# Attention heads in one hybrid decoder layer: where scores, values and filler work stand in TensorE's order, and how rotated queries and keys reach their tiles

## The chip, the cores and the metric

The kernel runs on one core of one Trainium2 chip. The metric is the device time of one execution in microseconds (us). Inputs and outputs lie in the chip's DRAM, the on-chip memory is called SBUF, and TensorE adds up its products in PSUM. The engines are named as in the profile: PE (TensorE), DVE (VectorE), ACT (ScalarE), POOL (GpSimd) and SP (SyncE). Here SP issues every DMA, one after the other in program order.

## The reference, cut to what matters

One decoder layer for 1024 tokens and width 1024. Its first sub-layer runs two mixers on the same input x and merges them; cross-attention and a feed-forward network follow. The part that the change touches is the second mixer, differential attention with 8 heads, two 64-wide query and key components per head, and 128-wide values:

```python
dq = rope(da_q, positions);  dk = rope(da_k, positions)      # (.., 8 heads, 2, 64)
lam = exp(sum(lam_q1*lam_k1)) - exp(sum(lam_q2*lam_k2)) + lam_init
# per head and block of 128 queries:
s = einsum('qcd,kcd->cqk', q, k) * 64**-0.5,  -inf above the diagonal
p = softmax(s, -1);  a = p[0] - lam * p[1];  o = a @ v
o = head_rms_norm(o, da_norm_w) * (1 - lam_init)
y_b = o @ w_proj_b
mix = (g_a * y_a + g_b * y_b) @ w_mix_out        # y_a: output of the first mixer times w_proj_a
```

## The kernel before

Every large product is made in three TensorE passes: an f32 operand is split into a high part (`bh`, `whi`) and a rest (`bl`, `wlo`), and high by high, rest by high and high by rest are added. ACT or POOL writes the high part, DVE or POOL the rest (`to_hi` and `to_lo`, lines 139 to 149); all matmuls are recorded at line 152.

PE follows the order in which the program is written (`manual_schedule`); the other engines' orders come from a scheduler. The written order is made by a small queue of generators, `Weave`. A filler (a piece of work that depends on nothing in the attention) is added to the queue and gives up control after each *quantum*, in most fillers three matmuls of 512 columns. The attention's own generator yields a number, and `W.pump(n)` then writes n quanta of filler behind what the attention has just written. `W.ensure(name)` writes filler until the named one is complete; `W.later` calls a function some quanta on. A head yields 60 quanta in all.

Per head, four groups g of 256 queries are done: `scores(h, g)` writes the products of Q with K and with klo (the rest of K) into PSUM tiles `sp`; DVE copies them into `e` with mask and row maximum (lines 679 and 682), turns the maximum into the bias of the exponential (L686), ACT takes the exponential and its sum, DVE inverts the sum and multiplies one half by -lam (L691), POOL scales one half of `e` (L692) and DVE joins both (L693). `values(h, g)` transposes `e` on PE (`tp`), ACT and DVE split the result into `ath` and `atl`, and PE multiplies with the values into `op`. Lines 736 to 750 then do the RMS norm: `of` is the scaled output (DVE, L741), a sum of squares `ss` goes through PE five quanta later, ACT takes Ln and Exp of it into `rt`, POOL multiplies, and a DMA writes `of` to `oT_d` in DRAM. `values(h, g-1)` follows `scores(h, g)`, and `values(h, 3)` stands directly behind `values(h, 2)`.

The fillers are listed per head in `FILL`: "P" the projections of the next head (`g_rope` for Q and K, per pair of heads also V), "G" a gate (`g_gate`), "q" and "v" cross-attention products that are spilled to DRAM (`spill`, tile `ev`, ACT at L765), "h" the loads of the first mixer's result hT into the buffers that held x (`g_load`, 16 DMAs of 512 KB), and "Y" its output projection y_a (eight `g_ya`, 16 quanta each). `g_rope` rotates a 128x512 block in tiles `raw` and `rot` (tag "rope", four buffers, shared with `gt`, `ev` and `vt`) and writes it from SBUF to SBUF into Q, K and klo, by DMAs of 64 partitions (L633). Each of Q, K and klo has two tiles and one buffer per tile. Before a head's first scores, `ensure` writes out what is left of its Q and K.

Behind the attention the last quanta of y_a are drained, while oT is loaded from `oT_d` and split (`load_slab`, 8 slabs of 512 KB); its products with w_proj_b (`yb`) come next.

Of the kernel before, what the change touches and what calls it, by code (L numbers as in the profile page):

```python
# [12 lines left out]
F = mybir.dt.float32  # L13
R = mybir.dt.float32r
I32 = mybir.dt.int32
AF = mybir.ActivationFunctionType
OP = mybir.AluOpType
# [13 lines left out]
BIG = 1e30  # L31
NEG = -1e30
# [3 lines left out]
NRAW = 4  # L36
AHEAD_T = 80
NG_A = 5
FILL = (("G", "q0", "P", "G"), ("P", "q1"), ("G", "q2", "P", "G"), ("P", "G"), ("G", "q3", "P", "G"), ("P", "G"),
        ("G", "P", "G"), ("h0", "v0", "h1", "v1", "h2", "v2", "h3", "v3", "Y"))  # L40
PUMP_K = 4
PUMP_S = 1
PUMP_T = 2
PUMP_O = 2
# [71 lines left out]
def hybrid_layer(ctx: ExitStack, tc: tile.TileContext, a: dict, out: bass.AP):  # L116
    nc = tc.nc
    V, S, G, PE = nc.vector, nc.scalar, nc.gpsimd, nc.tensor
# [9 lines left out]
    W = Weave()  # L128
# [5 lines left out]
    def to_hi(dst, src, eng=None):  # L134
        if eng is None:
            eng = hi_plan[turn["h"] % len(hi_plan)]
            turn["h"] += 1
        if eng == "s":
            S.activation(dst, src, AF.Copy)  # L139
        elif eng == "g":  # L140
            G.tensor_scalar(dst, src, 1.0, 0.0, op0=OP.mult, op1=OP.add)  # L141
        else:
            V.tensor_copy(dst, src)
# [47 lines left out]
    def g_fm(wsrc, acts, evac, pool=None, w=None):  # L191

        w = w or split_all(load_w(wsrc, pool), 1024, pool)
        for j, (ah, al) in enumerate(acts):
            n = ah.shape[-1]
            acc = acc_tile()
            for k in range(KT):
                mm3(acc[:, :n], cut(w[k // 4], (k % 4) * 128, (k % 4) * 128 + 128), (ah[:, k, :], al[:, k, :]),
                    k == 0, k == KT - 1)
                yield  # L200
            evac(j, acc)
# [38 lines left out]
    hT_d = dr.tile([2, 8, 128, 1024], F, name="hT_d")  # L240
    oT_d = dr.tile([8, 128, 1024], F, name="oT_d")
    g_d = dr.tile([16, 128, 1024], F, name="g_d")
    row_d = dr.tile([2, 32, 128], F, name="row_d")
    dec_d = dr.tile([1, 32], F, name="dec_d")

# [359 lines left out]
    with tc.tile_pool(name="bp", bufs=1, reuse_waits="tile") as B:  # L605
        def g_rope(h, which):


            t_ = 16 + 8 * which + h
            dst = [B.tile([128, 1024], R, tag=f"{'QK'[which]}{c}", name=f"{'QK'[which]}{c}") for c in range(2)]  # L610
            if which == 0:
                res["Q"] = dst
                to = [[(dst[0], 0), (dst[1], 64)], [(dst[0], 64), (dst[1], 0)]]
            else:
                klo = [B.tile([128, 1024], R, tag=f"klo{c}", name=f"klo{c}") for c in range(2)]
                res["K"], res["klo"] = dst, klo
                to = [[(kt, r) for kt in pr for r in (0, 64)] for pr in (dst, klo)]

            def ev(j, acc):
                js = slice(j * 512, (j + 1) * 512)  # L620
                raw = B.tile([128, 512], F, tag="rope", name="raw", bufs=NROPE)
                rot = B.tile([128, 512], F, tag="rope", name="rot", bufs=NROPE)
                S.activation(raw, acc, AF.Identity, bias=bfm[:, t_:t_ + 1])
                V.stream_shuffle(rot, raw, [i ^ 16 for i in range(32)])
                V.tensor_tensor(raw, raw, cosT[:, js], op=OP.mult)
                G.tensor_tensor(rot, rot, sinT[:, js], op=OP.mult)
                V.tensor_tensor(raw, raw, rot, op=OP.add)
                to_hi(rot.bitcast(R), raw, "s")
                V.tensor_tensor(raw.bitcast(R), raw, rot, op=OP.subtract)
                for m, places in zip((rot, raw), to):  # L630
                    for n, (t, r) in enumerate(places):
                        c = n if which == 0 else n // 2
                        dma(t[r:r + 64, js].bitcast(F), m[c * 64:c * 64 + 64])  # L633
            yield from g_fm(a["wfm"][t_], xT, ev)

        def g_vB(pr):
            bvd = B.tile([128, 256], F, tag="bvd", name="bvd", bufs=1)
# [13 lines left out]
            res["V", 2 * pr], res["V", 2 * pr + 1] = (vh[0], vl[0]), (vh[1], vl[1])  # L651

        def addB(h):
            if h % 2 == 0:
                W.add(f"V{h}", g_vB(h // 2))
            W.add(f"Q{h}", g_rope(h, 0))
            W.add(f"K{h}", g_rope(h, 1))

        def scores(h, g, qk):
            out_ = []  # L660
            for i in (2 * g, 2 * g + 1):
                n = (i + 1) * 128
                nch = 1 if n <= 512 else 2
                w0 = ((i + 1 + nch - 1) // nch) * 128
                cuts = [(0, w0)] if nch == 1 else [(0, w0), (w0, n)]
                e = [B.tile([128, 1024], F, tag=f"e{c}", name=f"e{c}", bufs=4 - 2 * c) for c in range(2)]
                mx = B.tile([128, 2], F, tag="mx", name="mx", bufs=3)
                su = B.tile([128, 2], F, tag="ssum", name="ssum", bufs=3)
                for c in range(2):
                    run = None  # L670
                    for j, (c0, c1) in enumerate(cuts):
                        w = c1 - c0
                        sp = sm_tile("sp")
                        qs = slice(i * 128, (i + 1) * 128)
                        mm(sp[:, :w], qk[0][c][:, qs], qk[1][c][:, c0:c1], start=True)
                        mm(sp[:, :w], qk[0][c][:, qs], qk[2][c][:, c0:c1], stop=True)
                        if j < len(cuts) - 1:
                            run = B.tile([128, 1], F, tag="run", name="run", bufs=2)
                            V.tensor_scalar(e[c][:, c0:c1], sp[:, :w], 1.0, None, op0=OP.mult, op1=OP.max,
                                            accum_out=run)  # L680
                        else:
                            V.tensor_tensor_reduce(e[c][:, c0:c1], sp[:, :w], cmask[:, 512 - w:512], scale=1.0,
                                                   scalar=NEG if run is None else run, op0=OP.add, op1=OP.max,
                                                   accum_out=mx[:, c:c + 1])
                        yield PUMP_S
                V.tensor_scalar(mx, mx, -0.125, None, op0=OP.mult)  # L686
                for c in range(2):
                    S.activation(e[c][:, :n], e[c][:, :n], AF.Exp, scale=0.125, bias=mx[:, c:c + 1],
                                 accum_out=su[:, c:c + 1])
                V.reciprocal(su, su)  # L690
                V.tensor_tensor(su[:, 1:2], su[:, 1:2], nlam, op=OP.mult)  # L691
                G.tensor_scalar(e[1][:, :n], e[1][:, :n], su[:, 1:2], 0.0, op0=OP.mult, op1=OP.add)  # L692
                V.scalar_tensor_tensor(e[0][:, :n], e[0][:, :n], su[:, 0:1], e[1][:, :n], op0=OP.mult, op1=OP.add)  # L693
                out_.append(e[0])
            res["a", h, g] = out_

        def values(h, g):
# [40 lines left out]
            to_hi(sqp[0], sq, "g")  # L738
            to_lo(sqp[1], sq, sqp[0], "v")
            of = B.tile([128, 256], F, tag="of", name="of", bufs=1)  # L740
            V.tensor_scalar(of, op_[:, :256], dag[:, h:h + 1], None, op0=OP.mult)  # L741
            def norm():
                ss = sm_tile("ss")
                mm(ss[:, :256], ones, sqp[0], start=True)
# [49 lines left out]
        gates = iter(range(NG_A, 16))  # L794

        def attention():
            for h in range(8):
                for nm in FILL[h]:
                    add_fill(nm, h)
                W.ensure(f"Q{h}")  # L800
                W.ensure(f"K{h}")
                W.pump(PUMP_K)
                qk = (res["Q"], res["K"], res["klo"])
                if h == 0:
                    with tc.issue_after(res["act"]), tc.issue_after(res["act2"]):
                        S.preload_act_table_set("natural_log_exp_and_others")
                for g in range(4):
                    yield from scores(h, g, qk)
                    if g > 0:
                        yield from values(h, g - 1)  # L810
                yield from values(h, 3)

        def g_load(part):
            if part == 0:
# [6 lines left out]
                        hT_d[i, ks, :, h * 512:(h + 1) * 512].rearrange("k p c -> p k c"))  # L821
            yield from ()

        def add_ya():
            for f in range(8):
                W.add(f"ya{f}", g_ya(f))

        def gate(i, pool, tag):
# [17 lines left out]
            dma(g_d[f], gt)  # L846

        def add_fill(nm, h):
            if nm == "G":
                W.add("g", g_gate(next(gates), B, "rope", NROPE))  # L850
            elif nm == "P":
                addB(h + 1)
            elif nm[0] == "h":
                W.add("hT", g_load(int(nm[1])))
            elif nm == "Y":
                add_ya()
            elif nm[0] == "q":
                W.add("q", g_qk(int(nm[1])))
            else:
                W.add("v", g_vo(int(nm[1])))  # L860

        addB(0)
        add_fill("G", 0)
        W.drain()
        for n in attention():
            W.pump(n)
        W.pump(LAG_O)
        W.flush()

# [559 lines left out]
```

## Time and profile before

| | |
|---|---|
| Median of 3 runs | 2286.19 us (2283.52 to 2288.44) |
| Profiled execution | 2285.06 us, its span 2283.3 us |
| Mean granted clock of TensorE | 0.989 |
| PE busy | 2207.3 us (97%) |
| DVE busy | 1421.2 us (62%) |
| ACT busy | 696.4 us (30%) |
| POOL busy | 704.9 us (31%) |

The span runs from the first to the last instruction. Busy time of PE includes matmuls whose modelled ends overlap the next one's start. The attention lies between about 450 and 1125 us of the span.

### The profile page before, as it was taken

How to read it: one execution, taken by the hardware profiler on the slowest of the kernel's cores; microseconds unless marked ns; L12 is line 12 of the kernel's file. 1: busy time of each engine (PE TensorE's matmuls, PEld its weight loads, DVE VectorE, ACT ScalarE, POOL GpSimd, SP SyncE). 2: the span in 40 equal slices, each digit the busy share in tenths (PEclk: the TensorE clock that was granted, in tenths of full speed). 3: DMA queues.
4: the chain of work that ended last, by engine and by line, in shares of the span. 5: the costliest groups of instructions: out<-in, count | busy, mean ns of one | idle time of the engine just before them, and what ended most of it. 6: DMA issues, size and time to landing. Idle time of an engine off the chain costs nothing.

```text
span 2283.3 us, 36224 instructions
## 1 busy us (share of the span) xinstructions
PE 2207.3 (97%) x14109; PEld 2008.0 (88%) x14109; DVE 1421.2 (62%) x2655; ACT 696.4 (30%) x1375; POOL 704.9 (31%) x720
## 2 busy tenths in 40 slices
PE   8999999999999999998999999997999999999997
PEld 8898898887988888886888999997899999999996
DVE  8536645357777676676535486478756665556657
ACT  3322213234454454445232123222211111111122
POOL 7124323233333332334412232245421111111124
PEclk9999999999999999999999999999999999999999
DMA  8322222344263343439733423222211111111122
GB/s 319 102 73 93 83 65 88 127 124 132 63 181 100 81 128 83 108 103 316 254 137 138 177 83 105 81 84 74 65 39 54 47 46 56 56 48 45 56 64 94
DMA packets 97963, 238.47 MB, mean 104 GB/s; under 512 B 12128, under 2 KB 30464, under 8 KB 97792
## 3 DMA queue, kind: packets, MB, share of 16 engines
q1 hardware_dynamic: 97792, 236.16, 32.5%
q8 instruction: 111, 1.82, 0.3%
q14 instruction: 60, 0.49, 0.1%
HBM read 168.92 MB, written 41.98 MB: 92 GB/s over the span
## 4 chain that ended last, share of the span: by engine, by line
PE 51%; DVE 5%; DMA 2%; issue 2%; POOL 1%; ACT 1%; SPq 0%; DVEq 0%; POOLq 0%; ACTq 0%
PE acc L152 32%; PE xb L152 7%; PE xa L152 5%; PE xc L152 5%; DVE wlo L149 1%; DMA vo_d<-ev 1%; PE sp L152 1%; DVE d L1040 1%; PE op L152 1%; DVE z L930 0%; DVE xb L149 0%; PE tp L722 0%; DVE z L926 0%; DVE u L1040 0%; PE tp L1007 0%
## 5 line engine op out<-in xcount | busy, mean ns | idle before, releaser
L141 POOL TENSOR_SCALAR whi<-wraw 128x512 fp32r<-128x512 f32 (+1 forms) x250 | 180.0, 720 | 880.3 <-issue 355.6
L152 PE MATMUL acc<-bh,whi 128*128 128x512 f32 x1024 | 418.1, 408 | 0.4 <-ACT gtok L389 0.4
L149 DVE TENSOR_TENSOR wlo<-wraw,whi 128x512 fp32r<-128x512 f32 (+1 forms) x379 | 306.3, 813 | 160.8 <-ACT whi L139 121.1
L152 PE MATMUL acc<-bh,wlo 128*128 128x512 f32 x1024 | 402.2, 393 | 0.0
L152 PE MATMUL acc<-bl,whi 128*128 128x512 f32 x1024 | 402.0, 393 | 0.0
L139 ACT ACTIVATE whi<-wraw 128x512 fp32r<-128x512 f32 (+1 forms) x252 | 157.4, 626 | 550.9 <-PE acc L152 273.9
L152 PEld LDWEIGHTS acc<-bh,wlo 128*128 128x128 f32 x1024 | 193.6, 189 | 42.5
L152 PEld LDWEIGHTS acc<-bh,whi 128*128 128x128 f32 x1024 | 194.0, 189 | 33.4 <-ACT gtok L389 0.6
L152 PEld LDWEIGHTS acc<-bl,whi 128*128 128x128 f32 x1024 | 194.3, 190 | 32.3
L152 PE MATMUL acc<-whi,bh 128*128 128x256 f32 (+1 forms) x728 | 213.2, 293 | 0.2 <-DVE ev L149 0.2
L152 PE MATMUL acc<-whi,bl 128*128 128x256 f32 (+1 forms) x728 | 205.6, 282 | 0.0
L152 PE MATMUL acc<-wlo,bh 128*128 128x256 f32 (+1 forms) x728 | 205.4, 282 | 0.0
L152 PE MATMUL xb<-xe,whi 128*128 128x256 f32 x1008 | 183.8, 283 | 10.3 <-DVE u L1040 7.4
L149 POOL TENSOR_TENSOR wlo<-wraw,whi 128x512 fp32r<-128x512 f32 (+1 forms) x125 | 174.1, 1393 | 9.8
L152 PEld LDWEIGHTS xb<-xe,whi 128*128 128x128 f32 x1008 | 155.9, 190 | 10.9 <-issue 6.8
L152 PE MATMUL xb<-xe,wlo 128*128 128x256 f32 x504 | 142.5, 283 | 0.0
L152 PEld LDWEIGHTS acc<-whi,bh 128*128 128x128 f32 x728 | 138.7, 190 | 2.0 <-DVE ev L149 0.4
L152 PEld LDWEIGHTS acc<-wlo,bh 128*128 128x128 f32 x728 | 138.7, 190 | 1.6
L152 PEld LDWEIGHTS acc<-whi,bl 128*128 128x128 f32 x728 | 138.6, 190 | 0.0
L1250 DVE SCALAR_TENSOR_TENSOR z<-z,acc 128x512 f32<-128x512 f32 x144 | 98.2, 685 | 53.4 <-PE acc L152 51.8
L152 PE MATMUL xa<-xb,whi 128*128 128x256 f32 x672 | 125.5, 287 | 5.2 <-ACT u L1162 5.2
L152 PE MATMUL acc<-wlo,hidh 128*128 128x512 f32 x320 | 124.7, 390 | 1.4 <-DVE wlo L149 1.4
(315 smaller groups left out, 5205.1 us busy)
## 6 DMA issues: line engine op xcount, KB each, us to landing
wraw<-in_wfm_dram SPq DMA_DIRECT2D x48, 512.0 KB, 3.6
wraw<-in_wg_dram SPq DMA_DIRECT2D x24, 512.0 KB, 3.6
wraw<-in_wu_dram SPq DMA_DIRECT2D x24, 512.0 KB, 3.5
wraw<-in_wd_dram SPq DMA_DIRECT2D x22, 512.0 KB, 3.5
hT_d<-hp SPq DMA_DIRECT2D x16, 512.0 KB, 2.8
g_d<-gt SPq DMA_DIRECT2D x32, 256.0 KB, 2.3
K<-rot SPq DMA_DIRECT2D x64, 128.0 KB, 2.3
klo<-raw SPq DMA_DIRECT2D x64, 128.0 KB, 2.3
```

The costliest lines, as they stand in the source:

```text
L139: S.activation(dst, src, AF.Copy)
L141: G.tensor_scalar(dst, src, 1.0, 0.0, op0=OP.mult, op1=OP.add)
L149: (V if eng == "v" else G).tensor_tensor(dst, src, hi.bitcast(F), op=OP.subtract)
L152: PE.matmul(o, l, r, start=start, stop=stop, skip_group_check=True)
L1040: V.tensor_tensor(dst, x_, y_, op=op)
L1250: V.scalar_tensor_tensor(zs, zs, ALPHA if q == 0 else 1.0, acc, op0=OP.mult, op1=OP.add)
```

## The change

- `values(h, 3)` is written behind `scores(h+1, 0)` of the next head instead of before it; only `values(7, 3)` stands alone at the end.
- `FILL` is dealt out anew: each head gets the quanta of its list, divided by 60, for each quantum that the attention yields (`share`), so that a list is used up about when its head ends. The v fillers move forward to heads 4 to 6, the hT loads and the first half of y_a to head 6, and the second half of y_a to head 7. `values(7, 3)` has a share of 0. Before, the queue stayed full until the end.
- `g_rope` writes `rot` and `raw` into a new DRAM tensor `rq_d` (two DMAs of 128x512 per block), and `load_qk(h)` reads Q, K and klo of a head back by 24 DMAs of 64x512, issued once the previous head's last scores are written.
- The scores are copied with a factor of -0.125 and a minimum, so that L686 goes; -lam is a second operand of POOL's instruction, so that L691 goes; `of` is written by ACT instead of DVE (L741).

```diff
-FILL = (("G", "q0", "P", "G"), ("P", "q1"), ("G", "q2", "P", "G"), ("P", "G"), ("G", "q3", "P", "G"), ("P", "G"),
-        ("G", "P", "G"), ("h0", "v0", "h1", "v1", "h2", "v2", "h3", "v3", "Y"))
-PUMP_K = 4
+FILL_0 = ("P0", "V0", "G0")
+FILL = (("P1", "P2", "q0", "G0"), ("V2", "P3", "q1", "G0"), ("P4", "q2", "G0", "G0"), ("V4", "P5", "q3", "G0"),
+        ("P6", "v0", "G0", "G0", "G0"), ("V6", "P7", "v1", "G0"), ("v2", "v3", "G0", "h0", "h1", "h2", "h3", "Y0"), ("Y4",))
+QUANTA = {"P": 32, "V": 32, "G": 16, "q": 8, "v": 8, "h": 0, "Y": 64}
+PUMPS = 60
...
                 to_hi(rot.bitcast(R), raw, "s")
+                dma(rq_d[h, which, 0][:, js], rot)
                 V.tensor_tensor(raw.bitcast(R), raw, rot, op=OP.subtract)
-                for m, places in zip((rot, raw), to):
-                    for n, (t, r) in enumerate(places):
-                        c = n if which == 0 else n // 2
-                        dma(t[r:r + 64, js].bitcast(F), m[c * 64:c * 64 + 64])
+                dma(rq_d[h, which, 1][:, js], raw)
...
+        def load_qk(h):
+            t = [[B.tile([128, 1024], R, tag=f"{n}{c}", name=f"{n}{c}") for c in range(2)] for n in ("Q", "K", "klo")]
+            for j in range(2):
+                js = slice(j * 512, (j + 1) * 512)
+                for n in range(3):
+                    for c in range(2):
+                        for r in range(2):
+                            part = r if n == 0 else n - 1
+                            dma(t[n][c][r * 64:r * 64 + 64, js].bitcast(F),
+                                rq_d[h, min(n, 1), part][c * 64:c * 64 + 64, js])
+            return t
...
-                V.tensor_scalar(mx, mx, -0.125, None, op0=OP.mult)
...
-                V.tensor_tensor(su[:, 1:2], su[:, 1:2], nlam, op=OP.mult)
-                G.tensor_scalar(e[1][:, :n], e[1][:, :n], su[:, 1:2], 0.0, op0=OP.mult, op1=OP.add)
+                G.tensor_scalar(e[1][:, :n], e[1][:, :n], su[:, 1:2], nlam, op0=OP.mult, op1=OP.mult)
...
-            V.tensor_scalar(of, op_[:, :256], dag[:, h:h + 1], None, op0=OP.mult)
+            S.activation(of, op_[:, :256], AF.Copy, scale=dag[:, h:h + 1])
...
+            late = None
+            qk = load_qk(0)
...
                 for g in range(4):
                     yield from scores(h, g, qk)
-                    if g > 0:
-                        yield from values(h, g - 1)
-                yield from values(h, 3)
+                    if g == 3 and h < 7:
+                        W.ensure(f"K{h + 1}")
+                        qk = load_qk(h + 1)
+                    if late:
+                        if late[1] == 0 and late[0]:
+                            W.ensure(f"V{late[0] // 2 * 2}")
+                        yield from values(*late)
+                    late = (h, g)
+                yield None
+            yield from values(*late)
...
-        for n in attention():
-            W.pump(n)
+        for n in steps:
+            if n is None:
+                h += 1
...
+                share = sum(QUANTA[nm[0]] for nm in FILL[h]) / PUMPS if h < 8 else 0
+                continue
+            left += n * share
+            W.pump(int(left))
+            left -= int(left)
```

Where PE passes from the last gate, which still reads x (`acc_10282`), to the first y_a (`acc_10382`, from `bh_10349`, which lies in x's buffers), the order after the change reads:

```order
L154 MATMUL acc_10282<-bh_82,whi_10227 128x512
L154 MATMUL acc_10282<-bl_83,whi_10227 128x512
L154 MATMUL acc_10282<-bh_82,wlo_10228 128x512
L154 MATMUL acc_10382<-bh_10349,whi_10374 128x512
L154 MATMUL acc_10382<-bl_10350,whi_10374 128x512
L154 MATMUL acc_10382<-bh_10349,wlo_10375 128x512
L154 MATMUL sp_10386<-K1_9672,Q1_9670 128x384
L154 MATMUL sp_10386<-klo1_9674,Q1_9670 128x384
```

Before, the last filler ahead of the first y_a (`acc_11018`) is the fourth v (`acc_10989`), not a gate:

```order
L152 MATMUL acc_10989<-whi_10911,kvh_10891 128x512
L152 MATMUL acc_10989<-wlo_10912,kvh_10891 128x512
L152 MATMUL acc_10989<-whi_10911,kvl_10892 128x512
L152 MATMUL op_10933<-ath_10958,vh_8895 128x256
L152 MATMUL op_10933<-atl_10959,vh_8895 128x256
L152 MATMUL op_10933<-ath_10958,vl_8897 128x256
L152 MATMUL op_10933<-ath_10958,vh_8895 128x256
L152 MATMUL op_10933<-atl_10959,vh_8895 128x256
L152 MATMUL op_10933<-ath_10958,vl_8897 128x256
L152 MATMUL acc_11018<-bh_10520,whi_11010 128x512
L152 MATMUL acc_11018<-bl_10521,whi_11010 128x512
```

The four v fillers, 32 quanta, no longer stand between x's last reader and hT's first. At the end of the last head, PE's order after the change holds `values(7, 3)` alone, here its last two products and the transposes between them:

```order
L154 MATMUL op<-ath,vh 128x256
L154 MATMUL op<-atl,vh 128x256
L154 MATMUL op<-ath,vl 128x256
L723 MATMUL tp<-ident,e_11221 128x128
L723 MATMUL tp<-ident,e_11268 128x128
L720 MATMUL tp<-ident,e_11268 128x128
L154 MATMUL op<-ath,vh 128x256
L154 MATMUL op<-atl,vh 128x256
L154 MATMUL op<-ath,vl 128x256
```

Before, the same place has filler of y_a (`acc`) on both sides of the transposes:

```order
L152 MATMUL op<-ath,vh 128x256
L152 MATMUL op<-atl,vh 128x256
L152 MATMUL op<-ath,vl 128x256
L722 MATMUL tp<-ident,e_10799 128x128
L722 MATMUL tp<-ident,e_10856 128x128
L719 MATMUL tp<-ident,e_10856 128x128
L152 MATMUL acc<-bh,whi 128x512
L152 MATMUL acc<-bl,whi 128x512
L152 MATMUL acc<-bh,wlo 128x512
L152 MATMUL acc<-bh,whi 128x512
```

Behind `values(7, 3)`, 18 quanta of y_a are left after the change; before, seven of the eight y_a were. On SP, the loads of the second head's Q, K and klo (numbers 5067 to 5072) now stand between the filler's writes of `rot` and `raw`:

```order
L637 DMA Q_5067<-rq_d 64x512
L623 DMA rq_d<-rot 128x512
L637 DMA Q_5067<-rq_d 64x512
L625 DMA rq_d<-raw 128x512
L637 DMA Q_5068<-rq_d 64x512 x2
L637 DMA K_5069<-rq_d 64x512
L637 DMA K_5070<-rq_d 64x512 x2
L637 DMA klo_5071<-rq_d 64x512 x2
L637 DMA klo_5072<-rq_d 64x512 x2
```

At the same place before, the blocks went from `rot` and `raw` into the tiles directly:

```order
L633 DMA Q_4274<-rot 64x512
L633 DMA Q_4275<-rot 64x512
L633 DMA Q_4274<-raw 64x512
L633 DMA Q_4275<-raw 64x512
L633 DMA K_4362<-rot 64x512 x2
L633 DMA K_4363<-rot 64x512 x2
L633 DMA klo_4364<-raw 64x512 x2
L633 DMA klo_4365<-raw 64x512 x2
```

After the change the twelve loads of the second half follow at once, and only behind them the next writes of `rot` and `raw`. Each load needs its tile free of the previous head's scores; what stands behind it on SP waits with it.

## Rows read from the trace of the kernel before

**Rows 1.** Busy time in stretches; behind it granted clock, DMA share, GB/s
```profile
core 0: us, PE busy (x) PEld busy (x) DVE busy (x) ACT busy (x) POOL busy (x), PEclk, DMA share, GB/s
450.00:1125.00 675.00, 642.02 (x3644) 560.02 (x3644) 455.77 (x1084) 301.94 (x642) 238.62 (x254) 0.98 0.46 134
950.00:975.00 25.00, 22.71 (x106) 19.05 (x106) 15.86 (x56) 11.27 (x29) 6.57 (x9) 0.93 0.53 140
1050.00:1075.00 25.00, 17.21 (x69) 13.18 (x68) 14.46 (x33) 10.79 (x21) 8.22 (x9) 0.86 0.99 351
1125.00:1400.00 275.00, 273.93 (x1752) 250.10 (x1752) 155.62 (x258) 70.71 (x113) 70.96 (x73) 1.00 0.41 143
```

**Rows 2.** What PE waited for, whole span: us in total, times, longest
```profile
PE tp L722 <- DVE e L693: 12.7, 7, 3.6
PE sp L152 <- DMA klo<-raw: 9.0, 7, 2.3
...
PE acc L152 <- ACT ev L765: 6.4, 1, 6.4
...
PE op L152 <- DVE atl L149: 3.7, 7, 1.6
```

**Rows 3.** PE timeline at three places: start, us, instruction, idle before
```profile
954.25 0.67 PE L152 MATMUL acc<-bh,whi 128*128 128x512 f32 x1
954.72 0.63 PE L152 MATMUL acc<-bl,whi 128*128 128x512 f32 x1
...
1068.43 0.79 PE L152 MATMUL acc<-whi,kvh 128*128 128x512 f32 x1 [6.37 <-ACT ev L765]
...
1130.26 0.39 PE L152 MATMUL acc<-bh,whi 128*128 128x512 f32 x1
1130.49 0.39 PE L152 MATMUL acc<-bl,whi 128*128 128x512 f32 x1
```

**Rows 4.** DVE instructions by line, 450 to 1125: busy, mean ns, idle before
```profile
L741 DVE TENSOR_SCALAR of<-op,dag 128x256 f32<-128x256 f32 x32 | 15.3, 477 | 13.1 <-ACT sq L736 11.0 <-POOL gt L837 2.1
L686 DVE TENSOR_SCALAR mx<-mx 128x2 f32<-128x2 f32 x64 | 13.9, 217 | 1.1
L691 DVE TENSOR_TENSOR ssum<-ssum,nlam 128x1 f32<-128x1 f32 x64 | 11.0, 171 | 1.4
```

**Rows 5.** SP timeline: DMA issues at three places
```profile
483.76 2.38 SPq L633 DMA_DIRECT2D K<-rot  x4
...
1054.36 0.46 SPq L820 DMA_DIRECT2D bl<-hT_d  x1
1054.86 0.53 SPq L820 DMA_DIRECT2D bh<-hT_d  x1
...
1057.27 4.89 SPq L766 DMA_DIRECT2D vo_d<-ev  x4
1063.11 0.36 SPq L820 DMA_DIRECT2D bh<-hT_d  x1
...
1067.26 0.36 SPq L820 DMA_DIRECT2D bl<-hT_d  x1
...
1103.01 0.32 SPq L750 DMA_DIRECT2D oT_d<-of  x1
...
1103.90 17.07 SPq L166 DMA_DIRECT2D wraw<-oT_d  x8
```

**Rows 6.** DMA issues: count, KB each, median us from issue to landing
```profile
K<-rot SPq DMA_DIRECT2D x64, 128.0 KB, 2.3
...
oT_d<-of SPq DMA_DIRECT2D x32, 128.0 KB, 1.8
```

**Rows 7.** ACT and DVE timelines at the end of the attention
```profile
1101.24 0.47 ACT L747 ACTIVATE rt<-ss,epsc 128x256 f32<-128x256 f32 x1 [3.33 <-PE ss L152]
...
1110.38 0.69 DVE L149 TENSOR_TENSOR bl<-wraw,bh 128x512 fp32r<-128x512 f32 x1 [1.91 <-ACT bh L139]
...
1126.13 2.80 DVE L149 TENSOR_TENSOR bl<-wraw,bh 128x512 fp32r<-128x512 f32 x2
```

More of the change, by code (lines that the diff above doesn't have):

```diff
@@ L242, in hybrid_layer @@
     g_d = dr.tile([16, 128, 1024], F, name="g_d")
+    rq_d = dr.tile([8, 2, 2, 128, 1024], F, name="rq_d")
     row_d = dr.tile([2, 32, 128], F, name="row_d")
@@ L609, in g_rope @@
             t_ = 16 + 8 * which + h
[L610 to L617, printed above, removed]
             def ev(j, acc):
@@ L653, in addB @@
         def addB(h):
-            if h % 2 == 0:
-                W.add(f"V{h}", g_vB(h // 2))
             W.add(f"Q{h}", g_rope(h, 0))
@@ L678, in scores @@
                             run = B.tile([128, 1], F, tag="run", name="run", bufs=2)
-                            V.tensor_scalar(e[c][:, c0:c1], sp[:, :w], 1.0, None, op0=OP.mult, op1=OP.max,
+                            V.tensor_scalar(e[c][:, c0:c1], sp[:, :w], -0.125, None, op0=OP.mult, op1=OP.min,
                                             accum_out=run)
                         else:
-                            V.tensor_tensor_reduce(e[c][:, c0:c1], sp[:, :w], cmask[:, 512 - w:512], scale=1.0,
-                                                   scalar=NEG if run is None else run, op0=OP.add, op1=OP.max,
+                            V.tensor_tensor_reduce(e[c][:, c0:c1], sp[:, :w], cmask[:, 512 - w:512], scale=-0.125,
+                                                   scalar=BIG if run is None else run, op0=OP.add, op1=OP.min,
                                                    accum_out=mx[:, c:c + 1])
                         yield PUMP_S
-                V.tensor_scalar(mx, mx, -0.125, None, op0=OP.mult)
                 for c in range(2):
-                    S.activation(e[c][:, :n], e[c][:, :n], AF.Exp, scale=0.125, bias=mx[:, c:c + 1],
+                    S.activation(e[c][:, :n], e[c][:, :n], AF.Exp, scale=-1.0, bias=mx[:, c:c + 1],
                                  accum_out=su[:, c:c + 1])
                 V.reciprocal(su, su)
-                V.tensor_tensor(su[:, 1:2], su[:, 1:2], nlam, op=OP.mult)
-                G.tensor_scalar(e[1][:, :n], e[1][:, :n], su[:, 1:2], 0.0, op0=OP.mult, op1=OP.add)
+                G.tensor_scalar(e[1][:, :n], e[1][:, :n], su[:, 1:2], nlam, op0=OP.mult, op1=OP.mult)
                 V.scalar_tensor_tensor(e[0][:, :n], e[0][:, :n], su[:, 0:1], e[1][:, :n], op0=OP.mult, op1=OP.add)
@@ L796, in attention @@
         def attention():
+            late = None
+            qk = load_qk(0)
+            with tc.issue_after(res["act"]), tc.issue_after(res["act2"]):
+                S.preload_act_table_set("natural_log_exp_and_others")
             for h in range(8):
[L798 to L806, printed above, removed]
                 for g in range(4):
                     yield from scores(h, g, qk)
-                    if g > 0:
-                        yield from values(h, g - 1)
-                yield from values(h, 3)
+                    if g == 3 and h < 7:
[8 more added lines that the diff above has]
+            yield from values(*late)
         def g_load(part):
@@ L822, in g_load, with add_ya @@
             yield from ()
-        def add_ya():
-            for f in range(8):
+        def add_ya(fs):
+            for f in fs:
                 W.add(f"ya{f}", g_ya(f))
@@ L848, in add_fill @@
         def add_fill(nm, h):
-            if nm == "G":
+            if nm[0] == "G":
                 W.add("g", g_gate(next(gates), B, "rope", NROPE))
-            elif nm == "P":
-                addB(h + 1)
+            elif nm[0] == "P":
+                addB(h)
+            elif nm[0] == "V":
+                W.add(nm, g_vB(h // 2))
             elif nm[0] == "h":
-                W.add("hT", g_load(int(nm[1])))
-            elif nm == "Y":
-                add_ya()
+                W.add("hT", g_load(h))
+            elif nm[0] == "Y":
+                add_ya(range(h, h + 4))
             elif nm[0] == "q":
-                W.add("q", g_qk(int(nm[1])))
+                W.add("q", g_qk(h))
             else:
-                W.add("v", g_vo(int(nm[1])))
-        addB(0)
-        add_fill("G", 0)
+                W.add("v", g_vo(h))
+        for nm in FILL_0:
+            add_fill(nm, int(nm[1]))
         W.drain()
-        for n in attention():
-            W.pump(n)
+        steps, share, left = attention(), 0.0, 0.0
+        h = 0
+        for nm in FILL[0]:
+            add_fill(nm, int(nm[1]))
+        share = sum(QUANTA[nm[0]] for nm in FILL[0]) / PUMPS
+        for n in steps:
+            if n is None:
+                h += 1
+                for nm in FILL[h] if h < 8 else ():
+                    add_fill(nm, int(nm[1]))
+                share = sum(QUANTA[nm[0]] for nm in FILL[h]) / PUMPS if h < 8 else 0
[3 more added lines that the diff above has]
+            left -= int(left)
         W.pump(LAG_O)
```

## The prediction

> **What bounds the kernel now.** I read the windows first. From 450 to 1125, where all of the change lies, PE is busy for 642.0 of 675.0 us and its clock is 0.98; right behind, from 1125 to 1400, it is busy for 273.9 of 275 at 1.00 [rows 1]. PE is the bound, and what the change can give is what PE loses in the attention: 33.0 us of idle time, and 2% of 675, 13.5 us, of clock. The idle time is understated: full-speed matmuls of 512 columns are listed with 0.39 us but start 0.23 apart (1130.26, 1130.49) [rows 3], so each gap is shown 0.16 short; the 22 waits of the second view make this 3.5 us. In all, 50 us.
>
> The second view is the table of what PE waited for [rows 2]. Its four rows hold 31.8 of the 33.0 us: the transposes for `e` (12.7, 7 times), the scores for klo (9.0, 7 times), one accumulator for the spill's copy (6.4), the products for `atl` (3.7, 7 times). The third is PE's timeline, for what a wait costs behind it: after the klo wait near 953 the matmuls start 0.47 us apart instead of 0.23, half speed, the lower of the two clock levels [rows 3], and the window 950 to 975 has a clock of 0.93, 1.75 us lost [rows 1]. A wait of about 2 us so costs nearly twice its length; one of under 1 us mostly only itself. The 6.4 us wait lies in 1050 to 1075, where the clock is 0.86, 3.5 us lost [rows 1].
>
> So I split the 50 us: 1050 to 1075 (the hT loads) 6.4 + 0.2 + 3.5 = 10; everything else, waits for `e`, klo and `atl` with their clock, 40.
>
> **The change part by part.** PE's instructions are the same in number and shape in both orders; only their places move. "PE work" below is what the order holds between two places, at the trace's spacing.
>
> *A. Lag, load ahead, fewer DVE operations.* `values(h, 3)` gets `scores(h+1, 0)` and its filler in front. That removes the place where `e` is needed soonest after it is asked for: a head's last group, of the longest rows. Its chain also loses two DVE hops (L686 217 ns, L691 171 ns) and DVE loses 13.9 + 11.0 + 15.3 = 40.2 us of 455.8 busy [rows 1, 4]. L741's 15.3 us go to ACT, which is busy for 302 of 675 [rows 1], behind the same square as before; I cost it at nothing. A head's K comes from DRAM a head after its rotation, so the klo wait on a block just rotated goes. The new loads start when the old head's last scores have been read and have 14.3 us of PE work (12.1 for one head) before the next scores; 24 issues at 0.5 to 0.6 us (K x4 in 2.38; hT 1054.36 to 1054.86) [rows 5] put the half that is needed first, 12 loads, at 6 to 7 us, plus 2.3 to land [rows 6]: about 10, in time. What is late next is `atl`, whose 3.7 us nothing here shortens. I take 4 us. Bounds: 2 (half of that) and 10 (that, three of the seven `e` waits at 1.8, and one half-speed stretch).
>
> *D. SP's queue.* The 24 loads wait on SP for the old head's tiles, and the filler's `rot` and `raw` writes wait behind them. Those tiles share four buffers with `ev`: at four boundaries (into heads 1, 2, 4, 6) a spill's copy needs a buffer whose write stands behind the block, so ACT, in order, stops, and PE runs out of accumulators. At the first of them 21 loads and the write stand between the last scores and the copy, and PE has 14.4 us of work. At 0.5 us a load the copy is done after 21 x 0.5 + 0.4 (issue) + 2.3 (landing) + 0.6 = 13.8 us, at 0.62 after 16.3: waits from 0 to 2 us, with half speed behind the longer ones. Four times 0 to 4 makes 0 to 16; I take 5, nearer the low end, because 0.5 to 0.6 is what the rows show, and DRAM sources rather the shorter (the hT pair).
>
> *B. The first y_a.* In the order the last gate, which reads x, now touches the first y_a, which reads hT from the same buffers. The first 4 of 16 loads can go while the gate's second half runs, the others only when PE is past it. Between 1063.11 and 1067.26 each waiting load was let go 1.38 us after the one before, at a DMA share of 0.99 [rows 1, 5]. y_a's k-block 4 needs 10 loads and stands 3.9 us of PE work behind the gate: 6 x 1.38 + some 1.6 for the last to land = 9.9, a wait of 6. Block 6 needs 4 more, 5.5 us, against 1.4 of PE work: another 4. Idle time 10, at two places, plus clock as in 1050 to 1075 (3.5) and a little more: 15. Before, the four v fillers stood here and the same loads cost 10. Bounds 8 (6 of the loads go early) and 20.
> The DMA share of 0.99 came with 351 GB/s [rows 1]. The Trainium skill ("DMA: Bandwidth & Descriptors", Specifications) gives ~358 GB/s as a core's HBM limit and 435 GB/s as the fabric ceiling. By the first a 512 KB load takes an estimated 1.46 us and B is about 1 us more; by the second 1.21 and B is 2 us less. The trace's 1.38 lies between, so neither figure decides, and I keep 1.38.
>
> *C. The end.* `values(7, 3)` has no filler: after each of four transposes PE waits for ACT's and DVE's split of about 0.6 to 0.7 us each, partly beside the previous product. I take 2.8, and 1 for `e`, which has less in front. Then 18 quanta, 12.3 us (54 matmuls at 0.227), cover the whole way to yb. Counted from the last `op` matmul: the sum of squares comes 5 quanta on, 3.4 us; Ln to the write's issue is 1.8 us (1101.24 to 1103.01) [rows 5, 7]; but `of` has one buffer, which ACT now fills only when the write before has landed (1.8 us) [rows 6], about 3 us: loads start at 8.4. Before, the first load was issued at 1103.90 and the last block of the first half was split by 1127.5 (half of 1126.13 + 2.80) [rows 5, 7], 23.6 us: split at 32.0. PE wants it 7 quanta into the first yb, at 12.3 + 4.8 = 17.1: 14.9 late. The slabs no longer share `wraw` and DVE with the weights of three y_a; I take off 2, so 12.9 of waits, spread over several blocks, with 3 of clock. C = 2.8 + 1 + 12.9 + 3 = 19.7. Before, all of it lay beside 75 us of y_a and cost nothing: 1125 to 1400 is full [rows 1]. Bounds 8 (the splits, freed of weights, run at the rate of a 512 KB load per 1.4 us) and 26.
> DVE's `bl` took 0.69 us at 1110.38 and 1.40 each at 1126.13, where POOL was splitting too [rows 7]. The Trainium skill ("GPSIMD Engine Reference", 1. Specifications) says that GpSimd shares its SBUF interfaces with VectorE and contends with its instructions of two SBUF inputs, which `bl` is. By that rule C's low end is out of reach, since POOL takes half of the `bh` and a quarter of the `bl`; with 0.69 throughout, the 16 splits would be shorter by an estimated 5 us. The two rows agree with the rule.
>
> **Sum.** After: 4 + 5 + 15 + 19.7 = 43.7 against 50 before: 6.3 us gained. The profiled execution took 2285.06 us (span 2283.3 and 1.8 around it), 1.1 below the median of 2286.19; so 2278.8 on its scale and about **2279** as a median.
>
> **Rivals.**
> *R2, the spreading works nearly in full.* A 3, D 0, B 8, C 10: 21 after, 29 gained, 2257. For it: all four rows of waits are aimed at, and in `load_slab` only DVE was seen busy with other work. Against: the y_a cover is 75 us before and 12.3 after, and hT's loads saturate the DMA engines.
> *R3, the load block stalls ACT (slower).* Mechanism: at the four boundaries of D the block is longer than PE's 14.4 us. It decides from about 0.55 us a load; four queued spill DMAs took 4.89 us, 1.22 each [rows 5], when the queues were full. At 0.75 the copy is done after 19.1 us: 4.7 of waiting and 1.7 of clock, 6.4, four times 26. Then 65 after, 15 lost, 2301. For it: 64 issues more, and each writes 64 partitions only. Against: the DMA share is 0.46 over the attention [rows 1].
> *R4, given back.* The waits for `e` are not a matter of order: POOL and DVE run other work in front of L692 and L693, so A stays at 10; with B 17, C 20 and D 4 that is 51 after and no change, 2286. It includes that lag and load ahead do their work, and C and B take it all.
>
> **How the numbers follow.** Forecast 0.46, R2 0.18, R3 0.17, R4 0.19. Two runs of this kernel can be told apart from about 0.2%, 4.6 us: faster is below 2281.6, slower above 2290.8. The forecast's own range, from B, C and D half-way to their bounds, is 2269 to 2289; three quarters of it count as faster, a quarter as the same. With R2, a third of R4 for each verdict: faster 0.46 x 0.75 + 0.18 + 0.06 = 0.59; same 0.12 + 0.06 = 0.18, with 0.03 for a mild R3 0.21; slower 0.14 + 0.06 = 0.20. The range of 8 in 10 takes in most of R2 and the mild side of R3: 2257 to 2297.
>
> **What would show it.** A: the row of transposes waiting for `e` falls below 4 us in total and the row of scores for klo is gone. D: a row of PE waiting for ACT's `ev`, up to four times; over 4 us each is R3. B: where the first y_a starts, two waits for DMA of `bh` or `bl`, 10 us together, with a clock under 0.9. C: behind the last `op`, waits for DVE `bl` or ACT `bh` of 11 to 15 us in total before and inside the first yb. Nothing behind the attention should differ. The forecast is wrong if B and C together come out outside 20 to 42 us, or if transposes still wait over 8 us for `e`.

## The result

| | median, us | range, runs | ratio to before, 95% interval |
|---|---|---|---|
| before | 2285.64 | 2283.52 to 2288.44, 4 | |
| after | 2321.54 | 2319.69 to 2324.98, 4 | 1.0158 (1.014 to 1.0176) |

The change makes the kernel 36 us slower. The forecast was 2279 us, with a range that ended at 2297.

The first view is again the windows, now of the kernel after (the columns are those of rows 1). The attention lasts longer here, since y_a is done within it, so four stretches stand for [rows 1]'s 450 to 1125:

```profile
450.00:1050.00 600.00, 564.14 (x3229) 495.10 (x3228) 359.74 (x775) 261.58 (x566) 201.50 (x209) 0.97 0.46 145
1050.00:1085.00 35.00, 24.53 (x100) 18.46 (x99) 10.42 (x24) 7.06 (x15) 4.12 (x6) 0.80 0.73 264
1085.00:1175.00 90.00, 89.59 (x467) 76.19 (x465) 51.75 (x121) 40.16 (x82) 24.74 (x30) 1.00 0.46 148
1175.00:1220.00 45.00, 36.61 (x159) 27.36 (x158) 24.00 (x27) 16.36 (x27) 20.22 (x21) 0.89 0.53 193
```

Idle time and clock make 54 us (35.9 + 0.03 x 600) in the first stretch, 17.5 (10.5 + 7.0) at the first y_a and 13 (8.4 + 5.0) at the end: 85 against 46.5 before by the same reading. That is 38 more; the spans differ by 34.6 (2317.9 and 2283.3).

The second view, what PE waited for from 450 to 1050, answers to [rows 2]:

```profile
PE acc L154 <- ACT ev L766: 23.7, 5, 6.6
PE op L154 <- DVE atl L151: 6.1, 9, 1.8
PE ss L154 <- POOL sqp L143: 1.7, 2, 1.1
PE acc L154 <- DVE wlo L151: 1.7, 2, 1.5
```

The two rows that the change aims at, transposes for `e` and scores for klo, are gone. In their place is one row that was not there before 1050: an accumulator waits for the spill's copy `ev`. Four windows around its four long waits give the price:

```profile
560.00:580.00 20.00, 14.90 (x80) 13.82 (x79) 11.36 (x25) 8.96 (x22) 6.86 (x8) 0.77 0.77 233
655.00:675.00 20.00, 14.06 (x78) 12.71 (x77) 9.13 (x22) 8.70 (x22) 7.09 (x8) 0.83 0.75 243
820.00:840.00 20.00, 13.38 (x71) 11.98 (x70) 10.72 (x24) 7.93 (x20) 7.10 (x8) 0.74 0.77 251
1000.00:1020.00 20.00, 14.87 (x63) 12.26 (x62) 9.35 (x24) 8.81 (x21) 7.01 (x8) 0.83 0.86 280
```

PE is busy for 57.2 of 80 us and its clock is 0.74 to 0.83: 22.8 idle and 16.6 of clock, 39 us, as much as the whole difference. The long waits are the one of 5.10 at 570.61, at the end of the next view, and these:

```profile
662.83 0.58 PE L154 MATMUL acc<-kvh,whi 128*128 128x256 f32 x1 [5.94 <-ACT ev L766]
...
829.42 0.58 PE L154 MATMUL acc<-kvh,whi 128*128 128x256 f32 x1 [6.62 <-ACT ev L766]
...
1007.18 0.80 PE L154 MATMUL acc<-whi,kvh 128*128 128x512 f32 x1 [5.13 <-ACT ev L766]
```

The timeline of all engines shows what stands in front of the first of the four (start, us, instruction, idle before and what ended it):

```profile
559.95 0.63 ACT L141 ACTIVATE rot<-raw 128x512 fp32r<-128x512 f32 x1 [4.53 <-DVE raw L621]
560.48 0.67 ACT L617 ACTIVATE raw<-acc,bfm 128x512 f32<-128x512 f32 x1
...
561.83 0.72 DVE L618 STREAM_SHUFFLE rot<-raw 128x512 f32<-128x512 f32 x1
562.33 2.51 SPq L637 DMA_DIRECT2D klo<-rq_d  x4
...
562.63 1.80 POOL L620 TENSOR_TENSOR rot<-rot,sinT 128x512 f32<-128x512 f32 x1 [4.84 <-DVE rot L618]
564.47 0.69 DVE L621 TENSOR_TENSOR raw<-raw,rot 128x512 f32<-128x512 f32 x1 [1.19 <-POOL rot L620]
564.93 0.67 SPq L623 DMA_DIRECT2D rq_d<-rot  x1
565.19 0.63 ACT L141 ACTIVATE rot<-raw 128x512 fp32r<-128x512 f32 x1 [4.04 <-DVE raw L621]
565.70 0.38 SPq L625 DMA_DIRECT2D rq_d<-raw  x1
...
567.59 1.75 DVE L151 TENSOR_TENSOR wlo<-wraw,whi 128x512 fp32r<-128x512 f32 x1
569.25 0.28 DVE L685 CUSTOM_DVE_ANT_0 e<-sp,cmask 128x128 f32<-128x128 f32 x1
...
569.58 0.40 ACT L690 ACTIVATE e<-e,mx 128x128 f32<-128x128 f32 x1 [2.60 <-DVE mx L685]
...
569.98 1.06 ACT L766 ACTIVATE ev<-acc 128x512 f32<-128x512 f32 x2
...
570.61 0.58 PE L154 MATMUL acc<-kvh,whi 128*128 128x256 f32 x1 [5.10 <-ACT ev L766]
```

Read it backwards. PE's matmul at 570.61 waits for the copy of 569.98. On ACT the copy stands behind the exponential of 569.58, which waits for a row maximum that DVE reaches only at 569.25, behind two splits; before that, ACT sat idle for 4.04 and 4.53 us in front of the high parts of two blocks of the rotation, the later one a chain ACT, DVE, POOL, DVE, ACT of 4.7 us from the projection's copy (560.48) to its high part (565.19). On SP the loads of Q, K and klo (2.51 for four, 0.63 each) end at 564.9, and only then go the writes that free the shared buffers. Such a write lands 2.0 us after its issue (median of 32), so an estimate puts the first free buffer at 566.9; the copy came 3 us later. Two causes offer themselves: SP's block (theory 1, the mechanism of R3) and the rotation's chain in ACT's and DVE's order, with the spills written right behind it (theory 2).

The trace has two more spills right behind a projection, q2 and v0, but with no block of loads beside them. At q2 ACT waited 0.92 us for the buffer and PE not at all for `ev`; at v0 PE's wait was 0.92 us:

```profile
718.33 0.60 ACT L766 ACTIVATE ev<-acc 128x512 f32<-128x512 f32 x1 [0.92 <-DMA rq_d<-rot]
...
889.47 0.50 PE L154 MATMUL acc<-bh,whi 128*128 128x512 f32 x1 [0.92 <-ACT ev L766]
```

In the kernel before, q1 stands behind a projection as well (its copy at 644.54 follows the high part of 644.00), and [rows 2] has no wait for `ev` there. So theory 2 alone made no long wait in either kernel.

### The profile page after: what moved, and what is told of

The parts are those of the page before. It is cut to its first block, busy times and chain, and to the rows that moved or that the text cites. A ratio compares the mean times of both kernels' runs of the same rounds, so it can differ in the third digit from the quotient of the medians.

```text
span 2317.9 us, 36076 instructions
## 1 busy us (share of the span) xinstructions
PE 2222.8 (96%) x14109; PEld 2016.1 (87%) x14109; DVE 1393.2 (60%) x2495; ACT 699.5 (30%) x1401; POOL 708.6 (31%) x720
## 4 chain that ended last, share of the span: by engine, by line
PE 81%; DVE 7%; issue 4%; POOL 3%; DMA 2%; ACT 1%; SPq 1%; DVEq 0%; POOLq 0%; ACTq 0%
PE acc L154 56%; PE xb L154 7%; PE xa L154 5%; PE xc L154 5%; PE sp L154 2%; PE op L154 2%; DVE wlo L151 2%; PE nm L154 1%; DMA bl<-hT_d 1%; POOL rot L620 1%; PE tp L723 1%; DVE d L1059 1%; POOL e L693 1%; SPq L637 1%; PE kv L154 1%
## 5 line engine op out<-in xcount | busy, mean ns | idle before, releaser
L690 ACT ACTIVATE e<-e,mx 128x256 f32<-128x256 f32 (+7 forms) x128 | 99.3, 775 | 131.0 <-DVE mx L685 130.6
```

The source lines that it names most:

```text
L690: S.activation(e[c][:, :n], e[c][:, :n], AF.Exp, scale=-1.0, bias=mx[:, c:c + 1], accum_out=su[:, c:c + 1])
```

## The experiments

Ratios are to the kernel before, measured again beside each run (its medians there 2285.2 to 2287.5).

**e1, spills ahead of the projections.** Only the order within the heads' lists changes.

```diff
-FILL = (("P1", "P2", "q0", "G0"), ("V2", "P3", "q1", "G0"), ("P4", "q2", "G0", "G0"), ("V4", "P5", "q3", "G0"),
-        ("P6", "v0", "G0", "G0", "G0"), ("V6", "P7", "v1", "G0"), ...
+FILL = (("q0", "P1", "P2", "G0"), ("q1", "V2", "P3", "G0"), ("q2", "P4", "G0", "G0"), ("q3", "V4", "P5", "G0"),
+        ("v0", "P6", "G0", "G0", "G0"), ("v1", "V6", "P7", "G0"), ...
```

> The changed kernel with q0, q1, q3 and v1 written ahead of the projections of their head instead of behind them. The four long waits of PE for ACT's ev cost 23.7 us and, with the half-speed stretches behind them, about 36. Theory 1 (the 24 loads of Q, K and klo hold back the writes of raw and rot, so the spill's copy gets its buffer late and its place on ACT too) and theory 2 (the spills stand directly behind a rotated projection, whose chain over ACT, DVE and POOL of nearly 5 us blocks ACT in order, whatever SP does) both expect about 36 us less, near 2286, and a row of PE waiting for ev under 3 us. If the time stays above 2310, the loss isn't at the spills.

2282.6 us, 0.9987 (0.9978 to 0.9997): 39 less than the change, and no row for `ev` from 450 to 1050. The loss is at the spills. A gate in their place fills an accumulator in 8 quanta instead of 2, which may be why a late copy is not felt there.

**e2, 12 loads of 128 partitions.** `dma(t[n][c][:, js], rq_d[h, min(n, 1), :, c*64:c*64+64, js])`, with one part read twice for K and klo.

> The changed kernel with 12 loads of 128x512 per head instead of 24 of 64x512 (the same bytes written; K and klo are duplicated within one DMA). Theory 1: the block of loads shrinks from 14 us to 6 or 7, the writes behind it go 7 us earlier, and the waits for ev fall from 23.7 us to under 6: 25 to 36 us less, 2286 to 2297. Theory 2: the chain of the rotation is what it was, the waits stay above 15 us, 2305 or more.

2647.37 us, 1.1584 (1.1563 to 1.1604). Neither theory is tested: the new form of DMA is slow by itself (a window, then SP's timeline).

```profile
575.00:635.00 60.00, 9.56 (x69) 8.61 (x67) 9.58 (x15) 3.30 (x8) 5.60 (x4) 0.62 0.19 69
...
579.19 5.10 SPq L638 DMA_DIRECT2D K<-rq_d  x1
584.34 5.07 SPq L638 DMA_DIRECT2D klo<-rq_d  x1
```

Here each held SP for 5 us, with the DMA engines busy for 0.19 of the time (first line). It says nothing on the four places.

**e3, buffers of its own for ev** (tag "ev", two; one each for `kvh` and `kvl`).

> The changed kernel with two buffers of their own for ev, which no longer shares the four of raw and rot (paid for by one buffer instead of two for kvh and kvl). The loads still take 14 us on SP. Theory 1: the copy no longer waits for SP's writes, the waits for ev nearly vanish at the four places, 28 to 36 us less, 2286 to 2294; the second half of a spill may wait for its own buffer's DMA behind the block, some us of that. Theory 2: 2305 or more.

2310.59 us, 1.0103 (1.0081 to 1.0126): 11 less than the change. The row for `ev` falls to 5.8 us, as theory 1 says, but the time follows only in part: waits for `sqp`, `wlo` and `atl` at the same places took over, and one wait of 4.9 us for `ev` is new, at v2 and v3, where `ev` now has two buffers instead of a share in four.

**e4, Q, K and klo loaded once.** `qk = load_qk(h + 1)` removed.

> The changed kernel that loads Q, K and klo once, for head 0, and uses them in every head: it leaves out the 168 loads of the seven other heads, so SP's blocks are gone and nothing else changes. Theory 1: waits for ev under 3 us, about 36 us less, 2286. Theory 2: waits for ev above 15 us, 2305 or more.

2306.01 us, 1.0084 (1.0065 to 1.0104): 15 less than the change, not 36. The row for `ev` is all but gone, as theory 1 says, and the time is that of theory 2. PE still waited 20 us from 450 to 1025, in pieces of 1.5 at most:

```profile
PE ss L154 <- POOL sqp L143: 6.5, 6, 1.4
PE op L154 <- DVE atl L151: 4.9, 7, 1.4
PE acc L154 <- DVE wlo L151: 3.2, 3, 1.5
PE ss L154 <- DVE sqp L151: 2.9, 6, 0.5
PE op L154 <- ACT ath L141: 1.5, 1, 1.5
PE acc L154 <- ACT ev L766: 0.9, 1, 0.9
```

The edit changed more than SP: the scheduler, which fixes ACT's order before the run, put the first copy of the spill ahead of the rotation's high part (in e3 too):

```profile
562.48 0.60 ACT L766 ACTIVATE ev<-acc 128x512 f32<-128x512 f32 x1 [1.57 <-DMA rq_d<-rot]
564.95 0.63 ACT L141 ACTIVATE rot<-raw 128x512 fp32r<-128x512 f32 x1 [1.87 <-DVE raw L621]
```

So e3 and e4 take away the wait for the buffer and the place behind the exponential together.

**e13 and e14, without the rotation.** In `g_rope` only ACT's copy with the bias and the two writes are left; e14 takes e4's loads out too. PE's instructions are the same.

```diff
-                V.stream_shuffle(rot, raw, [i ^ 16 for i in range(32)])
...
-                dma(rq_d[h, which, 0][:, js], rot)
-                V.tensor_tensor(raw.bitcast(R), raw, rot, op=OP.subtract)
+                dma(rq_d[h, which, 0][:, js], raw)
```

> The changed kernel without the rotation: it leaves out the shuffle, the products with cosine and sine, the sum and the split, and writes the projection itself to both parts of rq_d, so that ACT, DVE and POOL have one instruction per block instead of seven; the 24 loads per head stay on SP, PE's order too. Theory 1 (SP's block holds the shared buffers): the stores still wait behind the loads, the spills still wait for ev, no more than 15 us less than the changed kernel, 2306 or more. Theory 2 (the rotation's chain, in order on ACT, DVE and POOL, stands in front of the spills): 20 us or more less, 2285 to 2300. Both at work: between, near 2300.

> e13 without the loads of heads 1 to 7 as well (e4's edit). If block and chain together make up what e1 took away (39 us), the time is near e1's, 2278 to 2286; if something third stands at the spills (the short waits for sqp and atl), it stays above 2292.

e13: 2266.01 us, 0.9916 (0.9893 to 0.9939), 55 less than the change. Its window from 450 to 1050, loads and all:

```profile
450.00:1050.00 600.00, 590.15 (x3424) 519.33 (x3423) 283.93 (x669) 263.05 (x562) 151.16 (x188) 0.99 0.51 164
```

PE is busy for 590 us where it was for 564, and the row for `ev` is gone. e14: 2268.97, 0.9926 (0.9905 to 0.9946): without the rotation the loads cost nothing. With the loads out in both, the rotation is worth 37 us (e4 to e14); with the rotation in both, the loads are worth 15 (after to e4).

These sums are over the whole kernel. PE's order is the same in the changed kernel and in e3, e4, e13 and e14, so the same matmuls can be timed in each. Four stretches of the changed kernel hold the four places: 550 to 590, 645 to 690, 810 to 850 and 990 to 1030. Their matmuls take 17 us less in e3, 21 in e4 and 41 in e13 as in e14. (e4's profiled execution, 2300.75 us, lies 5 below its median.) At the four places, then, the block is worth about half of the 41 us while the rotation is there, and nothing without it. The rest of e13's 55 us lies elsewhere.

So the cause is three things at one place: a block of loads, the rotation and a spill behind it. Without the block the wait for `ev` and about half of the loss go (e3, e4), without the spill (e1) or the rotation (e13) all of it. Not shown is what about the rotation does it. e13 takes away the chain, 76 us of DVE's work (359.7 to 283.9 busy in this window) and half of the use of the shared buffers at once: at the first place the spill's copy no longer waits for a buffer, only for PE.

```profile
555.57 0.60 ACT L759 ACTIVATE ev<-acc 128x512 f32<-128x512 f32 x1 [1.45 <-PE acc L154]
```

**e7, the kernel before with the smaller vector work alone.** The order, the filling and the rotation's way are those of before.

```diff
-                V.tensor_scalar(mx, mx, -0.125, None, op0=OP.mult)
...
-                V.tensor_tensor(su[:, 1:2], su[:, 1:2], nlam, op=OP.mult)
...
-            V.tensor_scalar(of, op_[:, :256], dag[:, h:h + 1], None, op0=OP.mult)
+            S.activation(of, op_[:, :256], AF.Copy, scale=dag[:, h:h + 1])
```

> The kernel before with the smaller vector work alone (L686 and L691 gone, of written by ACT); order, filling and rotation as before. Theory: the chain of e is two hops and some 0.4 us shorter and DVE 9% less busy, so the waits of the transposes for e fall from 12.7 to 7 to 10 us, and 2 to 6 us of time go: 2280 to 2284. Rival: the waits for e are those for one another in POOL's and DVE's order, nothing changes, 2285 to 2288.

2268.19 us, 0.9919 (0.9905 to 0.9932): 18 less than before, three times the most that was expected. What PE waited for from 450 on:

```profile
PE sp L152 <- DMA klo<-raw: 8.8, 7, 2.1
PE acc L152 <- ACT ev L763: 6.4, 1, 6.4
PE op L152 <- DVE atl L149: 1.6, 5, 0.6
...
PE tp L720 <- DVE e L691: 0.3, 1, 0.3
```

Against [rows 2] the waits for `e` fall from 12.7 to 0.3 us, and those for `atl` from 3.7 to 1.6. Behind the two longest waits for `e` (2.72 and 3.58 us) PE also ran at half speed for a stretch (granted clock 0.57 from 551 to 555 and from 698 to 702); behind the one of 2.64 at 1006 it did not (1.00). No run separates the three cuts.

**e8, e1 without the smaller vector work.**

> e1 with the vector work of the kernel before (L686 and L691 back, of on DVE). Theory: with the lag across heads e is there in any case, so the time stays within 4 us of e1 (2279 to 2287) and the row of transposes waiting for e stays under 2 us. Rival: the lag alone doesn't hide the longer chain; waits for e come back with 5 us or more, and 2288 to 2296.

2280.1 us, 0.9975 (0.9966 to 0.9985), no slower than e1, and no row of transposes for `e`. The lag (with the rest of the change) and the shorter chain cure the same wait, and either one is enough.

**e10, the lag alone, on e7.** `yield from values(*late)` behind the next scores, across heads.

> e7 with the lag across heads alone: values(h, 3) behind scores(h+1, 0); filling and rotation as before. Theory: e7's transposes hardly wait for e any more (0.3 us), so the lag has nothing to give: 2265 to 2272. Rival: the lag fills the place of the klo wait with something or takes filler from the end: 2258 to 2262, or above 2274 if V's buffers are then late.

2282.99 us, 0.9984 (0.9973 to 0.9995): 15 more than e7.

```profile
PE sp L152 <- DMA klo<-raw: 14.7, 12, 2.4
PE acc L152 <- ACT ev L763: 6.9, 2, 6.5
```

The waits for klo grow from 8.8 to 14.7. The lag has nothing left to give and makes the scores more often late; why they are, no run settles.

**e9, the klo wait hidden by filler, on e7.** `PUMP_K = 4` becomes 8.

> e7 (the kernel before with the smaller vector work) with 8 instead of 4 quanta of filler ahead of each head's first scores. In e7 the scores wait 8.8 us for klo at 7 heads, 1.3 to 2.1 each, with half speed behind four of them, about 17 us in all. Theory: the block just rotated is only 1 to 2 us late, so 2.7 us of filler hide it without the way through DRAM: the row falls under 1 us and the time by 9 to 15, to 2253 to 2260. Rival: the four quanta are missing later in the head and the waits come back as waits for e or atl: within 4 us of e7, 2264 to 2272.

2254.4 us, 0.9862 (0.9849 to 0.9875): 14 less than e7, and the lowest time of all. The row for klo is gone.

```profile
450.00:1125.00 675.00, 663.70 (x3785) 578.98 (x3784) 432.33 (x939) 327.49 (x688) 250.79 (x264) 0.99 0.49 147
```

PE is busy for 663.7 us against 642.0 in [rows 1]. What is left is mostly one wait of 7.1 us for `ev` at the hT loads.

**e5 and e6, the other two terms, on e1.** e5 has head 6 in the order gate, h0, v2, h1, h2, v3, h3, y_a; e6 deals 14 quanta less out in head 7.

> e1 with head 6's list in the order gate, h0, v2, h1, h2, v3, h3, y_a, so that 16 quanta of v stand between the last reader of x and the first reader of hT. e1 loses about 14 us there (waits for bh and bl of hT 9.8 us, the rest half speed). Theory: the wait is the time that 16 loads of 512 KB take; with 11 us of filler beside them it falls to 3 to 6, 8 to 11 us less than e1, near 2273. Rival: the spills of v2 and v3 queue behind the loads on SP, and a wait for ev takes the place of the other, as in the kernel before (6.4 us); then no more than 4 us less, 2279 to 2283.

> e1 with 14 quanta fewer dealt out in head 7, so that 32 instead of 18 are left behind the last values (9.5 us more of cover). e1 loses about 16 us from the last values to the first yb. Theory: the chain from the last sum of squares over oT's writes and loads to its split is longer than the 18 quanta; the waits for bl (7.0 us) and their half speed go, 8 to 11 us less, near 2273. Rival: head 7, with a third less filler, waits for its own atl and e instead: within 3 us of e1.

e5: 2281.49, 0.9977 (0.9967 to 0.9986), 1 less than e1; PE still waits 7.7 us for `bh` of hT, whose last loads are issued behind the stores of v2 and v3. The rival's time holds, but not by a wait for `ev`, which is 0.5 us. e6: 2278.26, 0.9966 (0.9954 to 0.9979), 4 less; the waits for `bl` fall from 7.0 to 2.6 us. The theory holds for half of its size.

**e11 and e12, q2 and q3 into head 7,** on e7 and on e9.

> e7 with q2 and q3 moved from heads 2 and 4 into head 7, between the hT loads, so that 48 instead of 32 quanta lie between the last reader of x and y_a. e7 loses 12 us there, 6.4 of it one wait for ev, whose stores queue behind hT's loads at a full DMA queue. Theory: with 11 us more of filler the loads need a smaller share of the queue; the wait goes, 6 to 10 us less, 2258 to 2262. Rival: two more spills put more stores behind the same loads, and the wait stays, 2266 to 2272.

> e9 and e11 together: the sum of what each gives over e7, 2243 to 2255 if both theories hold; 2264 or more if neither does.

2283.41, 0.9988 (0.9979 to 0.9996), and 2268.09, 0.9924 (0.991 to 0.9937): 15 and 14 more than without. The wait for `ev` splits into three that sum to the same 6.4, and one of 10.0 for DVE's `gt` comes near the end of the attention. A miss: what e11 took away at one place came back at another, and why `gt` is late, no run settles.

## Why the prediction was wrong

**Step D failed: 5 us forecast, 39 measured.** The place was named, four boundaries where the copy `ev` is late, and R3 carried the sign. The sum for one boundary, 21 loads + 0.4 + 2.3 + 0.6, counted the copy as if it ran as soon as its buffer was free, with loads at 0.5 us. At the measured 0.63 us a load it gives 16.5 us and a wait of 2.1; the four waits were 5.1 to 6.6. Left out was ACT's own order: the copy stood behind a block of the rotation, for whose high part ACT waits 4 us, and behind an exponential that waits for DVE, so that it came some 3 us after its buffer was free. Left out as well was what lies behind the wait for `ev`: with the block gone, waits for `sqp`, `wlo` and `atl` at the same places kept half of the loss (e4); they went with the rotation (e13). The order of the fillers, which the prediction did not weigh, brought block, rotation and spill to one place; e1 undoes it with only the order of the lists changed. In the trace of before, q1 stood behind a projection without harm, with no block of loads on SP.

By the prediction's own sign, waits for `ev` of over 4 us at up to four places, this was R3, and R3's condition, more than about 0.55 us a load, held. R3's price failed too: it took loads of 0.75 us and came to 26; they kept to 0.63, and the rest of the 39 is what R3 left out as D did. The two signs by which the forecast was to count as wrong did not show: B and C together came to 30.5 us, and no transpose of the attention waited for `e`. They looked at the terms that were right.

**Step A: 4 us forecast, about 15 measured** (the first stretch's 54 without the four windows' 39). The rows for `e` and klo went, as forecast. The short waits did not stay at `atl`'s 3.7 but came to 6.1, with `sqp`, `wlo` and `ath` beside it. The mechanism had a wrong weight too: the lag was taken to do most, and e7 shows that the two small DVE instructions and `of` do it without the lag, 18 us by themselves.

**Step B, the first y_a, was right:** 15 forecast, 17.5 measured. The idle time was 10.5 where 10 was forecast, two waits for `bh` and four for `bl`; the clock, 0.80, cost 7.0 where 5 was taken.

```profile
PE acc L154 <- DMA bh<-hT_d: 8.5, 2, 6.9
PE acc L154 <- DMA bl<-hT_d: 2.0, 4, 0.7
```

**Step C, the end, was right in kind:** 19.7 forecast, 13 measured; the waits for `bl` are 7.0 us where 11 to 15 were named. The bare `values(7, 3)` costs next to nothing: 90 us up to 1175 are full, and behind that only 0.9 us of waits are for `atl` and `ath`.

```profile
PE acc L154 <- DVE bl L151: 7.0, 6, 2.4
PE op L154 <- DVE atl L151: 0.6, 2, 0.3
...
PE op L154 <- ACT ath L141: 0.3, 1, 0.3
```

One reading in C is weaker than it was put: POOL began a `bl` of its own at 1110.47, beside the `bl` of 0.69 us at 1110.38. A split of 0.69 us with POOL idle is the one at 1107.78 (`wlo`).

The sum by these steps is 85 for 43.7. 34 of the 41 missing are D.

## What to carry over

When filler is dealt out anew, follow the first instructions behind each place where one filler gives way to the next, on every engine, not only on the one that is filled: an eviction (the copy that empties an accumulator) is as late as the buffer that it needs and as whatever stands before it in its engine's order. Put work that fills accumulators quickly away from a block of DMAs and from work with a long vector chain that shares its buffers. And try the small cuts in a chain alone first: here they gave 18 us and four quanta at the right place 14 more, while the large rearrangement as a whole was slower than before.

## What was not expected of the hardware

A load of 128 partitions made of two groups of 64 rows (128x1x512 in e2) took 0.5 us to issue behind a pause (568.28) but held SP for about 5 us once several stood in the queue, and the queue moved 69 GB/s with the DMA engines 0.19 busy (575 to 635). In the changed kernel a load of 64x512, half as large, took 0.63 us with the engines 0.69 busy (550 to 567). The cause was not looked into. Around the waits of 5 to 6.6 us the granted clock was 0.74 to 0.83 over 20 us: each place lost about 4 us of clock on top of 5.7 us of idle time.
